# Stick-breaking decode over a paged cache: values fetched by quarter pages from GpSimd's queue, attention weights turned on TensorE

## The chip, the cores and the metric

One core of one Trainium2 chip runs the whole program. The metric is the device time of one execution in microseconds (us), median of three runs. The engines are PE (TensorE: matmuls, with PEld for its weight loads), DVE (VectorE), ACT (ScalarE), POOL (GpSimd), and SP, which here only issues DMAs. SPq, ACTq and POOLq are the queues of those engines' sequencers, from which DMAs are issued.

## The reference

One step of a hybrid decoder layer, for a prompt of 1024 tokens and for 8 samples of 8 new tokens each, whose past is 4096 tokens in a paged cache. Half of the heads do native sparse attention (NSA), the other half stick-breaking attention. The change touches the stick-breaking part of the samples alone:

```python
def stick_breaking(q, q_pos, k, v, k_pos):
    z = jnp.einsum('bqhd,bkhd->bhqk', q, k).astype(jnp.float32) * (HEAD_DIM ** -0.5)
    before = (k_pos[None, :] < q_pos[:, None])[None, None]
    log_beta = jnp.where(before, jax.nn.log_sigmoid(z), -jnp.inf)
    log_keep = jnp.where(before, jax.nn.log_sigmoid(-z), 0.0)
    log_keep_after = lax.cumsum(log_keep, axis=3, reverse=True) - log_keep
    a = jnp.exp(log_beta + log_keep_after)
    return jnp.einsum('bhqk,bkhd->bqhd', a, v.astype(jnp.float32)).astype(q.dtype)
```

`cache_sb` has 320 pages of 128 tokens; a token has 8 heads of 64 keys (2 KB) and then 8 heads of 64 values (2 KB). A sample's page table names its 32 pages, so 8 samples read 256 pages, 134 MB in all.

## The kernel before

The program goes through four stages: the projections with the prompt's stick-breaking attention (to about 590 us of the profiled span), the samples' NSA (to about 970 us), then the prompt's NSA together with the samples' stick-breaking attention (about 976 to 1520 us), and the output projections. The change lies in the third of these, in `phase_b`.

`phase_b` makes 32 steps, 4 for each sample, from the last token backwards (the cumulative sum runs in reverse, and a step hands its carry to the next). A step covers 8 pages, that is two halves `f` of four pages. Its parts are functions of the class `Step`, each with a due time in `BSTEP`, counted in steps:

- `load` (L1472): one DMA of SP for a page, keys and values together (512 KB), into a slot of the tile `bkv`. There are 8 slots for keys (`K.nkk`) and 24 for values (`K.nkv`), from the list `BC`. A load waits until both of its slots are free.
- `turn` (L1484): DVE transposes the 32x32 blocks of one page of keys (128x512) into `bkT`.
- `score` (L1491): 128 small matmul records on PE for the scores `bz` of a step, 32 columns at a time in four tile positions.
- `soft` (L1499): softplus on ACT and DVE, a scan on DVE for each half of the heads (L1507 calls L1407), the carried offsets by two matmuls into `bpt` (L1515, L1516; the PSUM pool holds one such buffer, `K.npt`), a subtraction on POOL (L1522), and the exponential on ACT (L1524).
- `out` (L1527): DVE turns the weights' 32x32 blocks (`baT`, L1531), then 16 copies of 32x128 elements, 8 on ACT and 8 on POOL, move the blocks between partition groups into `bAT` (L1539, L1541), and `av` (L1413) multiplies them with the values, page by page, into `bo`. These matmuls set the value slots free.

The prompt's NSA runs between these parts: 64 units (4 pairs of heads by 2 heads by 8 blocks of queries), each with scores on PE (L1037, L1210, L1217), a biased maximum on DVE (L1201), exponentials on ACT (L1221, L1235), three scalings by the gates (L1247), transposes on PE (L1256), copies out of PSUM on ACT (L1765) and the product with the values (L1279). `DSC` names the engine of the three scalings: "GGG" is POOL for all three, in the order selected, compressed (128x32, the tile `cz`), window. The letter list `MSB` holds no engine, so the framework orders each engine's queue in this stage by itself from the order of the program and its own estimates; on every engine the instructions then run in that order, and one that waits holds up all that is behind it. SP's queue holds the loads of all pages and a few loads and stores of the other parts.

Of the kernel before, what the change touches and what calls it, by code (L numbers as in the profile page):

```python
# [1322 lines left out]
def phase_b(K, es, psb):  # L1323

    nc, A, T = K.nc, K.A, K.T
# [57 lines left out]
    V.memset(one, 1.0)  # L1385
    vnew = cst.tile([32, 2, 512], F32, name="bvn")
# [3 lines left out]
    st = {}  # L1390
# [25 lines left out]
    carried, out, summed, count = {}, {}, [], [0]  # L1416
# [49 lines left out]
    class Step:  # L1466
# [5 lines left out]
        def load(t, i):  # L1472

            c = t.b * 32 + t.s * 8 + i
            n = count[0]
            count[0] += 1
            ks, vs = n % K.nkk, K.nkk + n % K.nkv
            t.k[i], t.v[i] = kv[:, ks], kv[:, vs]
            e = nc.sync
            with K.tc.issue_after(st[e].ins) if e in st else nullcontext():  # L1480
                r = e.value_load(pti[0:1, c:c + 1], min_val=0, max_val=319)
            st[e] = e.dma_start(kv[:, ks:vs + 1:vs - ks], cache[bass.ds(r, 1)].rearrange("o t (x c) -> (o t) x c", x=2))

        def turn(t, i):  # L1484
            f = i // 4
            if f not in t.kT:
                t.kT[f] = wT.tile([128, 16, 4, 32], F32, name="bkT", bufs=K.nkT)
            V.transpose(t.kT[f][:, :, i % 4], t.k[i].rearrange("p (j c) -> p j c", j=16))  # L1488
            t.done.append(("t", i))
# [9 lines left out]
        def soft(t):  # L1499

            assert ("s", 0) in t.done
            z, carry = t.z, carried[t.b]

            spc = wk.tile([128, 2, 257], F32, name="bs", bufs=2)
            sp = spc[:, :, 0:256]
            S_.copy(spc[:, :, 256:257], carry)
            t.a = a = wk.tile([128, 2, 256], F32, name="ba", bufs=2)  # L1507
            yield from softplus(a, sp, z)
            for g in range(2):
                scan(sp[:, g, ::-1], 256, spc[:, g, 256:257])  # L1510
            carried[t.b] = spc[:, :, 0:1]
            yield

            o = psb.tile([128, 512], F32, name="bpt", bufs=K.npt)[:, 0:16].rearrange("p (g k) -> p g k", g=2)
            nc.tensor.matmul(o, UL[0], sp[:, :, 0::32], start=True, stop=False, skip_group_check=True)  # L1515
            nc.tensor.matmul(o, UL[1], spc[:, :, 32::32], start=False, stop=True, skip_group_check=True)  # L1516
            V.tensor_tensor(a, z, sp, op=OP.subtract)
            yield
            os = wk.tile([128, 2, 8], F32, name="bos", bufs=2)
            S_.copy(os, o)  # L1520
            a4 = a.rearrange("p g (k t) -> p (g k) t", k=8)
            G.tensor_tensor(a4, a4, os.rearrange("p g k -> p (g k)").unsqueeze(2).to_broadcast([128, 16, 32]), op=OP.subtract)  # L1522
            yield
            S_.activation(a, a, AF.Exp)  # L1524
            t.done.append("w")

        def out(t):  # L1527

            assert "w" in t.done
            aT = wk.tile([128, 16, 32], F32, name="baT", bufs=1)  # L1530
            V.transpose(aT, t.a.rearrange("p g (k t) -> p (g k) t", k=8))  # L1531
            yield

            AT = wk.tile([128, 16, 4, 8], F32, name="bAT", bufs=2)
            for h in range(4):
                for x in range(4):
                    o, i = AT[x * 32:x * 32 + 32, :, h], aT[h * 32:h * 32 + 32, :, x * 8:x * 8 + 8]
                    if K.bev[(h * 4 + x) % len(K.bev)] == "A":
                        S_.copy(o, i)  # L1539
                    else:  # L1540
                        G.tensor_scalar(o, i, 1.0, 0.0, op0=OP.mult, op1=OP.add)  # L1541
            for f in (1, 0):
                yield
                for i in range(f * 4 + 3, f * 4 - 1, -1):
                    av(out[t.b // 4][:, t.b % 4], lambda g, hp: AT[:, g * 8 + i, hp * 2:hp * 2 + 2].rearrange("k h q -> k (h q)"), t.v[i],
                       False, t.s == 0 and i == 0)
                    summed.append(t.b // 4)
# [14 lines left out]
    for b in range(8):  # L1562
        g = begin(b)
        L += [(b * 4 + t, g) for t in P["b"]]
        for n in range(4):
            x = Step(b, 3 - n)
            t1 = b * 4 + n
            for m in range(8):
                L.append((t1 + P["k"][0] + m * P["k"][1], once(x.load, 7 - m)))
                L.append((t1 + P["t"][0] + m * P["t"][1], once(x.turn, 7 - m)))  # L1570
            for m in range(2):
                L.append((t1 + P["s"][m], once(x.score, 1 - m)))
            for name, g in (("w", x.soft()), ("x", x.out())):
                L += [(t1 + t, g) for t in P[name]]
# [157 lines left out]
BC = [int(x) for x in "1,1,8,24,2".split(",")]  # L1732
# [5 lines left out]
DSC = "GGG"  # L1738
# [10 lines left out]
BSTEP = {'k': [-1.2, 0.1], 't': [-0.35, 0.065], 's': [-0.08, 0.2], 'w': [0.22, 0.4, 0.56, 0.68, 0.78], 'x': [0.84, 0.9, 1.14, 1.24], 'n': [-1.6, -0.9, -0.85, -0.8, -0.78, -0.7, -0.65, -0.6], 'b': [-0.38, 1.05], 'f': [4.4]}  # L1749
# [178 lines left out]
```

## Time and profile before

| | before |
|---|---|
| median of 3 runs | 1796.08 us (1794.98 to 1798.1) |
| the profiled execution | 1797.21 us, its span 1795.4 us |
| PE busy | 1623.3 us, 90% of the span |
| DVE busy | 1233.7 us, 69% |
| ACT busy | 884.1 us, 49% |
| POOL busy | 613.5 us, 34% |

The span runs from the first to the last instruction that the profiler saw; the device time of the same execution is 1.8 us longer. Busy shares are averages over stages with different limits, so the stage of the change has to be read by itself. A group of instructions is given as line, engine, operation, output<-input, shape and count, then its busy time and the mean of one in ns, then the idle time of the engine just before and what ended it.

### The profile page before, as it was taken

Reading aid. Unit: us, or ns where it says so; the run is one execution under the profiler, and the core shown is the slowest. Engines: PE = TensorE matmul, PEld = TensorE weight load, DVE = VectorE, ACT = ScalarE, POOL = GpSimd, SP = SyncE. Lnnn points to the kernel's source line nnn. Section 1 sums busy time; section 2 is a strip of 40 time slices with the busy share of each in tenths; the row PEclk is TensorE's granted clock in tenths of the full one; section 3 lists DMA queues with packets and bytes.
Section 4 is the critical chain, followed back from the end, with each engine's and each line's share of the span. In section 5 each row is a group of like instructions: output and inputs, shape, how many; then the busy total and the mean of one; then the engine's idle time right before and its main releaser. Section 6 shows DMA issues by size and latency. Waiting matters only on the chain.

```text
span 1795.4 us, 41675 instructions
## 1 busy us (share of the span) xinstructions
PE 1623.3 (90%) x15742; PEld 1380.5 (77%) x15742; DVE 1233.7 (69%) x2892; ACT 884.1 (49%) x2220; POOL 613.5 (34%) x1057
## 2 busy tenths in 40 slices
PE   5999999999988799999998689898789898889998
PEld 5999898888876688899897466666567666677887
DVE  7336656877777578888887887877787785664322
ACT  4214645756657334444444467676567677311111
POOL 3123021121314455555553244344335444530000
PEclk9999999999987899999998699999799999799999
DMA  5235232131225455555555997876888872652210
GB/s 196 84 113 156 66 114 77 48 118 53 85 58 129 150 204 191 188 201 186 192 201 156 325 321 253 286 266 224 284 297 273 272 267 75 188 174 60 87 50 35
DMA packets 187082, 300.79 MB, mean 168 GB/s; under 512 B 30265, under 2 KB 100730, under 8 KB 178554
## 3 DMA queue, kind: packets, MB, share of 16 engines
q1 hardware_dynamic: 144930, 206.65, 35.5%
q0 software_dynamic: 9216, 67.11, 11.2%
q10 hardware_dynamic: 32736, 24.38, 4.3%
q8 instruction: 124, 2.03, 0.5%
q14 instruction: 76, 0.62, 0.1%
HBM read 271.81 MB, written 30.48 MB: 168 GB/s over the span
## 4 chain that ended last, share of the span: by engine, by line
PE 58%; DVE 14%; DMA 12%; issue 7%; ACT 5%; POOL 3%; SPq 1%; ACTq 0%; POOLq 0%; DVEq 0%
PE acc L278 12%; PE acc L1634 11%; PE H L510 6%; DMA bkv<-in_cache_sb 4%; PE bo L1413 4%; PE pt L1279 3%; DMA raw<-in_cache_nsa,cidx 3%; PE acc L276 3%; PE pt L1256 2%; PE bz L1397 2%; DVE bkT L1488 2%; PE pt L1106 2%; PE sc L682 2%; PE cav L824 1%; PE pt L1050 1%
## 5 line engine op out<-in xcount | busy, mean ns | idle before, releaser
L278 PE MATMUL acc<-whi,hh 128*128 128x256 f32 (+1 forms) x704 | 203.1, 290 | 4.1 <-DVE og L1767 2.5
L278 PE MATMUL acc<-wlo,hh 128*128 128x256 f32 (+1 forms) x704 | 200.7, 287 | 0.0
L278 PE MATMUL acc<-whi,hl 128*128 128x256 f32 (+1 forms) x704 | 199.7, 289 | 0.0
L1488 DVE STREAM_TRANSPOSE bkT<-bkv 128x512 f32<-128x512 f32 x256 | 170.4, 690 | 42.0 <-DMA bkv<-in_cache_sb 30.3
L278 PEld LDWEIGHTS acc<-whi,hh 128*128 128x128 f32 x704 | 134.5, 191 | 6.8 <-POOL whi L122 2.9
L491 ACT CAST XH<-xt 128x512 fp32r<-128x512 f32 x128 | 79.1, 618 | 121.8 <-PE H L510 111.1
L1247 POOL TENSOR_SCALAR t<-t,nst 128x640 f32<-128x640 f32 (+7 forms) x128 | 93.5, 732 | 129.5 <-DVE nst L1238 67.3
L278 PEld LDWEIGHTS acc<-wlo,hh 128*128 128x128 f32 x704 | 134.5, 191 | 0.2 <-issue 0.2
L278 PEld LDWEIGHTS acc<-whi,hl 128*128 128x128 f32 x704 | 132.3, 191 | 0.4 <-issue 0.3
L122 POOL TENSOR_SCALAR whi<-wraw 128x512 fp32r<-128x512 f32 (+1 forms) x60 | 53.8, 921 | 190.8 <-PE acc L248 154.7
L1413 PE MATMUL bo<-bkv,bAT 128*16 128x128 f32 x2048 | 93.6, 299 | 26.9 <-POOL bAT L1541 22.0
L1256 PE MATMUL pt<-idf,t 128*128 128x128 f32 x528 | 93.7, 294 | 18.0 <-ACT aT L1765 5.1
L661 POOL DMA_INDIRECT raw<-in_cache_nsa,cidx x64 | 66.9, 1045 | 102.9 <-DVE xt L486 51.1
L1541 POOL TENSOR_SCALAR bAT<-baT 32x128 f32<-32x128 f32 x256 | 75.4, 295 | 77.3 <-DVE baT L1531 54.0
L1765 ACT COPY aT<-pt 128x512 f32<-128x512 f32 (+3 forms) x167 | 77.0, 475 | 47.2 <-PE pt L1050 20.7
L1413 PEld LDWEIGHTS bo<-bkv,bAT 128*16 128x16 f32 x2048 | 62.6, 104 | 48.9 <-POOL bAT L1541 32.2
L1397 PE MATMUL bz<-bkT,bQ 128*32 128x128 f32 x2048 | 94.5, 293 | 4.0 <-DVE bkT L1488 1.3
L1256 PEld LDWEIGHTS pt<-idf,t 128*128 128x128 f32 x528 | 60.3, 146 | 44.2 <-issue 19.4
L510 PE MATMUL H<-w1hk,XH 128*128 128x256 f32 (+1 forms) x272 | 86.3, 317 | 8.6 <-ACT XH L491 7.8
L486 DVE STREAM_TRANSPOSE xt<-raw 128x512 f32<-128x512 f32 x132 | 88.1, 680 | 6.1 <-PE H L510 3.5
L1094 DVE TENSOR_TENSOR_SCAN t<-ones,t 128x1024 f32<-128x1024 f32 (+7 forms) x64 | 87.5, 1368 | 0.7
L496 POOL TENSOR_TENSOR XL<-xt,XH 128x512 fp32r<-128x512 f32 x56 | 72.1, 1287 | 37.2 <-ACT XH L491 36.6
(468 smaller groups left out, 5063.8 us busy)
## 6 DMA issues: line engine op xcount, KB each, us to landing
bkv<-in_cache_sb SPq DMA_DIRECT2D x256, 512.0 KB
wraw<-in_w_in SPq DMA_DIRECT2D x28, 512.0 KB
x<-in_x_prompt SPq DMA_DIRECT2D x8, 512.0 KB
out_sb_rows_prompt<-o ACTq DMA_DIRECT2D x32, 128.0 KB
s_gT<-og ACTq DMA_DIRECT2D x16, 256.0 KB
cwin<-in_state_win SPq DMA_DIRECT2D x8, 512.0 KB
wr<-in_w_out SPq DMA_DIRECT2D x16, 256.0 KB
u<-s_uT SPq DMA_DIRECT2D x8, 512.0 KB
```

The lines of the kernel that those rows point to most:

```text
L278: nc.tensor.matmul(acc[:, :w], a[:, k, t * 128:(t + 1) * 128], b[:, k, :w], start=i == 0, stop=i == 23)
L486: V.transpose(xt[:, :, e, :, b], raw[:, :, 0:256].rearrange("p l (k e c) -> p e l k c", e=2, c=32)[:, e])
L491: S_.copy(XH.rearrange("p a b -> p (a b)"), x.rearrange("p e k b s -> p (e k b s)"))
L510: nc.tensor.matmul(H[:m, kv * 256:kv * 256 + 256], x[:, c], y[:, l * 2 + e], start=start and l + kv + e + i == 0, stop=stop and l == 7 and ...
L1094: nc.vector.tensor_tensor_scan(a[:, ::-1], K.ones.to_broadcast([128, W]), a[:, ::-1], 0.0, op0=OP.mult, op1=OP.add)
L1247: nc.gpsimd.tensor_scalar(x, x, c, 1.0, op0=OP.mult, op1=OP.mult)
L1256: nc.tensor.transpose(pt[:, b * 128:(b + 1) * 128], x, K.id)
L1397: nc.tensor.matmul(z(h, g), q(j), kT(j), start=jj == 0, stop=jj == 1, skip_group_check=True, tile_position=(0, h * 32))
L1413: nc.tensor.matmul(oav[i * 32:i * 32 + 16], lhs(g, hp), v[:, i * 128:i * 128 + 128], start=first, stop=last, skip_group_check=True, tile_p ...
L1488: V.transpose(t.kT[f][:, :, i % 4], t.k[i].rearrange("p (j c) -> p j c", j=16))
L1634: nc.tensor.matmul(acc, a, b, start=i == 0, stop=i == len(terms) - 1)
L1765: S_.copy(o, i)
```

## The change

The page's values no longer come with its keys. SP loads only keys (256 KB a page). POOL gathers the values by indirect DMA, by quarter: one gather takes 32 tokens of each of the four pages of a half step, 128 rows of 2 KB, with row numbers computed once at the start of the stage (four small matmuls, a scaling and four DVE instructions for `vidx`). With values in that layout, the weights need a full 128x128 turn: four PE transposes a step into a `bpt` buffer and one ACT copy out of it replace the DVE turn and the 16 block copies. Keys are turned two pages at a time. One scan of 514 columns, with a mask `keep` that is zero where the second half begins, replaces two of 256. There are 12 slots for keys and 20 for values, keys are due 0.1 step earlier, values have due times of their own ("v"), and the scaling of the compressed part moves from POOL to DVE.

```diff
+    keep = cst.tile([128, 2, 257], BF, name="bkeep")
+    G.memset(keep, 1.0)
+    G.memset(keep[:, :, 256:257], 0.0)
+
+    vtab = hbm(A["cache_sb"], 0, [[512, 320 * 128 * 2], [1, 512]])
+    vidx = cst.tile([128, 4, 64], I32, name="bvi")
+    o32 = wk.tile([1, 32], F32, name="bu", bufs=2)
+    G.memset(o32, 1.0)
+    ptf = wk.tile([1, 256], F32, name="ba", bufs=2)
+    S_.copy(ptf, pti)
+    pp = psb.tile([128, 512], F32, name="bpt", bufs=K.npt)
+    for i in range(4):
+        nc.tensor.matmul(pp[i * 32:i * 32 + 32, 0:64], o32, ptf[:, i::4], start=True, stop=True, skip_group_check=True, tile_position=(0, i * 32))
+    vf = wk.tile([128, 64], F32, name="ba", bufs=2)
+    V.tensor_scalar(vf, pp[:, 0:64], 128.0, rq[:, 0:1], op0=OP.mult, op1=OP.add)
+    for x in range(4):
+        V.tensor_scalar(vidx[:, x], vf, 2.0, float(x * 64 + 1), op0=OP.mult, op1=OP.add)
...
-    carried, out, summed, count = {}, {}, [], [0]
+    carried, out, summed, count = {}, {}, [], [0, 0]
...
-            ks, vs = n % K.nkk, K.nkk + n % K.nkv
-            t.k[i], t.v[i] = kv[:, ks], kv[:, vs]
+            ks = n % K.nkk ^ 1
+            t.k[i] = ks
...
-            st[e] = e.dma_start(kv[:, ks:vs + 1:vs - ks], cache[bass.ds(r, 1)].rearrange("o t (x c) -> (o t) x c", x=2))
+            st[e] = e.dma_start(kv[:, ks], cache[bass.ds(r, 1)].rearrange("o t (x c) -> (o t) x c", x=2)[:, 0])
+
+        def values(t, m):
+
+            f, x = 1 - m // 4, m % 4
+            t.v[f, x] = v = kv[:, K.nkk + count[1] % K.nkv]
+            count[1] += 1
+            n = t.b * 8 + t.s * 2 + f
+            with K.tc.issue_after(st[G].ins) if G in st else nullcontext():
+                G.indirect_dma_start(out=v, out_offset=None, in_=vtab, in_offset=bass.IndirectOffsetOnAxis(ap=vidx[:, x, n:n + 1], axis=0))
...
-            V.transpose(t.kT[f][:, :, i % 4], t.k[i].rearrange("p (j c) -> p j c", j=16))
-            t.done.append(("t", i))
+            k = t.k[i]
+            assert i % 2 == 0 and k % 2 == 0 and t.k[i + 1] == k + 1
+            V.transpose(t.kT[f][:, :, i % 4:i % 4 + 2].rearrange("p j i t -> p i j t"), kv[:, k:k + 2].rearrange("p i (j c) -> p i j c", j=16))
+            t.done += [("t", i), ("t", i + 1)]
...
-            for g in range(2):
-                scan(sp[:, g, ::-1], 256, spc[:, g, 256:257])
+            x = spc.rearrange("p g c -> p (g c)")[:, ::-1]
+            V.tensor_tensor_scan(x, keep.rearrange("p g c -> p (g c)")[:, ::-1], x, 0.0, op0=OP.mult, op1=OP.add)
...
-            G.tensor_tensor(a4, a4, os.rearrange("p g k -> p (g k)").unsqueeze(2).to_broadcast([128, 16, 32]), op=OP.subtract)
+
+            st[G] = G.tensor_tensor(a4, a4, os.rearrange("p g k -> p (g k)").unsqueeze(2).to_broadcast([128, 16, 32]), op=OP.subtract)
...
-            aT = wk.tile([128, 16, 32], F32, name="baT", bufs=1)
-            V.transpose(aT, t.a.rearrange("p g (k t) -> p (g k) t", k=8))
-            yield
-
-            AT = wk.tile([128, 16, 4, 8], F32, name="bAT", bufs=2)
-            for h in range(4):
-                for x in range(4):
-                    o, i = AT[x * 32:x * 32 + 32, :, h], aT[h * 32:h * 32 + 32, :, x * 8:x * 8 + 8]
-                    if K.bev[(h * 4 + x) % len(K.bev)] == "A":
-                        S_.copy(o, i)
-                    else:
-                        G.tensor_scalar(o, i, 1.0, 0.0, op0=OP.mult, op1=OP.add)
+            pt = psb.tile([128, 512], F32, name="bpt", bufs=K.npt)
+            for f in (1, 0):
+                for g in range(2):
+                    c = f * 2 + g
+                    nc.tensor.transpose(pt[:, c * 128:c * 128 + 128], t.a[:, g, f * 128:f * 128 + 128], K.id)
+            yield
+
+            AT = wk.tile([128, 2, 2, 4, 4, 8], F32, name="bAT", bufs=2)
+            S_.copy(AT.rearrange("k f g x h q -> k (f g) h x q"), pt.rearrange("k (c h x q) -> k c h x q", c=4, h=4, x=4))
             for f in (1, 0):
                 yield
-                for i in range(f * 4 + 3, f * 4 - 1, -1):
-                    av(out[t.b // 4][:, t.b % 4], lambda g, hp: AT[:, g * 8 + i, hp * 2:hp * 2 + 2].rearrange("k h q -> k (h q)"), t.v[i],
-                       False, t.s == 0 and i == 0)
+                for x in range(4):
+                    av(out[t.b // 4][:, t.b % 4], lambda g, hp: AT[:, f, g, x, hp * 2:hp * 2 + 2].rearrange("k h q -> k (h q)"), t.v[f, x], False, t.s == 0 and f == 0 and x == 3)
...
-                L.append((t1 + P["t"][0] + m * P["t"][1], once(x.turn, 7 - m)))
+                L.append((t1 + P["v"][0] + m * P["v"][1], once(x.values, m)))
+                if m % 2:
+                    L.append((t1 + P["t"][0] + m * P["t"][1], once(x.turn, 7 - m)))
...
-BC = [int(x) for x in "1,1,8,24,2".split(",")]
+BC = [int(x) for x in "1,1,12,20,2".split(",")]
...
-DSC = "GGG"
+DSC = "GVG"
```

In `BSTEP`, 'k' goes from [-1.2, 0.1] to [-1.3, 0.1], and 'v': [-0.2, 0.12] is new; the other entries stay.

## Rows read from the trace of the kernel before

**Rows 1.** Busy time by stretch: whole stage, its start, two stretches with PE full:

```profile
core 0: us, PE busy (x) PEld busy (x) DVE busy (x) ACT busy (x) POOL busy (x), PEclk, DMA share, GB/s
985.00:1520.00 535.00, 454.49 (x6569) 340.60 (x6570) 416.40 (x1124) 366.36 (x1075) 221.12 (x504) 0.92 0.78 264
985.00:1060.00 75.00, 50.16 (x821) 38.07 (x824) 65.87 (x176) 39.83 (x118) 22.68 (x58) 0.75 0.99 340
1060.00:1080.00 20.00, 20.00 (x305) 14.65 (x295) 16.89 (x48) 15.86 (x44) 6.42 (x15) 1.00 0.74 252
1360.00:1400.00 40.00, 39.98 (x570) 29.59 (x569) 29.66 (x83) 29.27 (x87) 18.03 (x41) 0.99 0.89 302
```

**Rows 2.** Chain of work that ended last, 985 to 1520 us, shares by line:

```profile
by line: DMA bkv<-in_cache_sb 13.2%; PE bo L1413 11.8%; PE pt L1279 10.2%; PE pt L1256 8.2%; PE bz L1397 8.0%; DVE bkT L1488 6.8%; issue 3.9%; ACT bAT L1539 3.8%; POOL bAT L1541 3.4%; PE z L1210 3.4%; DVE t L1201 3.3%; PE z L1037 2.3%; DVE 
```

**Rows 3.** The same chain in order of time (start, us, what), 1140 to 1175 us:

```profile
1140.06 0.60 DVE baT L1531
...
1140.84 0.29 POOL bAT L1541
...
1143.34 0.31 POOL bAT L1541
1143.65 0.04 issue
1143.69 2.90 PE bo L1413 x62
...
1153.39 0.07 SPq L1482
...
1154.29 6.99 DMA bkv<-in_cache_sb
1161.28 0.02 issue
1161.31 0.71 DVE bkT L1488
```

**Rows 4.** Waits in the stage: total us, times, longest:

```profile
SPq L1482 <- PE bo L1413: 126.0, 43, 11.0
SPq L1482 <- DVE bkT L1488: 12.5, 9, 3.6
PE bo L1413 <- POOL bAT L1541: 22.0, 20, 5.5
PE bo L1413 <- ACT bAT L1539: 3.1, 5, 0.9
ACT ba L1524 <- POOL ba L1522: 8.3, 7, 3.0
```

**Rows 5.** Groups of instructions by shape, 985 to 1520 us:

```profile
L1488 DVE STREAM_TRANSPOSE bkT<-bkv 128x512 f32<-128x512 f32 x254 | 169.1, 690 | 41.9 <-DMA bkv<-in_cache_sb 30.3 <-PE bz L1397 10.7
L1256 PE MATMUL pt<-idf,t 128*128 128x128 f32 x483 | 84.4, 288 | 10.1 <-ACT aT L1765 4.6 <-ACT u L1765 1.7 <-ACT aW L1765 1.1
L1541 POOL TENSOR_SCALAR bAT<-baT 32x128 f32<-32x128 f32 x256 | 75.4, 295 | 77.3 <-DVE baT L1531 54.0 <-DVE nst L1238 6.0 <-DVE nst L1232 1.5
L1539 ACT COPY bAT<-baT 32x128 f32<-32x128 f32 x256 | 75.4, 294 | 12.4 <-DVE baT L1531 9.2
L1407 DVE TENSOR_TENSOR_SCAN bs<-bone,bs 128x256 f32<-128x256 f32 x64 | 46.1, 762 | 0.2
L1522 POOL TENSOR_TENSOR ba<-ba,bos 128x512 f32<-128x512 f32 x32 | 33.6, 1050 | 95.7 <-DVE nst L1232 31.4 <-ACT bos L1520 22.4 <-DVE ba L1517 16.6
L1765 ACT COPY aT<-pt 128x512 f32<-128x512 f32 x44 | 24.6, 578 | 13.9 <-PE pt L1256 13.7
L1531 DVE STREAM_TRANSPOSE baT<-ba 128x512 f32<-128x512 f32 x32 | 22.2, 694 | 6.9 <-ACT ba L1524 6.8
L1247 POOL TENSOR_SCALAR cz<-cz,nst 128x32 f32<-128x32 f32 x61 | 19.0, 311 | 0.0
```

**Rows 6.** DVE groups of other lines, whole span:

```profile
L715 DVE STREAM_TRANSPOSE cwT<-ckz 128x256 f32<-128x256 f32 x8 | 3.5, 437 | 0.0
L1094 DVE TENSOR_TENSOR_SCAN t<-ones,t 128x512 f32<-128x512 f32 x8 | 9.7, 1213 | 0.1
L346 DVE TENSOR_SCALAR cidf<-ptf,crv 128x32 f32<-128x32 f32 x2 | 0.8, 418 | 0.0
L347 DVE TENSOR_SCALAR cidx<-cidf 128x32 int32<-128x32 f32 x2 | 0.3, 174 | 0.0
```

**Rows 7.** Instructions of L661, the samples' NSA gather: ns min/median/max, first and last start:

```profile
L661 POOL DMA_INDIRECT raw<-in_cache_nsa,cidx x64: 937/988/2747, 568.3 to 948.4; - x64
...
DMA to landing us min/median/max: 5.6/6.0/8.2
```

More of the change, by code (lines that the diff above doesn't have):

```diff
@@ L1746 @@
 CHAIN = {'v': [-1.805], 'f': [3.581], 'q': [1.762, 2.274, 2.335, 2.335], 'k': [2.6, 2.7, 4.243, 4.243, 4.243, 4.342, 4.535, 4.559, 4.709, 4.909, 4.979, 5.109], 'w': [3.893, 4.152, 4.422], 'm': [5.22, 5.307, 5.457, 5.588, 5.688, 5.763, 5.924, 5.94, 6.122, 6.122], 's': [6.24, 6.31, 6.443, 6.443, 6.541, 6.635, 6.773, 6.935, 6.984], 'o': [6.868, 6.89, 6.977, 6.977, 7.127, 7.149, 7.151, 7.151, 7.151], 'p': [6.185, 6.243], 'z': [7.121, 7.181, 7.466, 7.643, 8.081]}
-BSTEP = {'k': [-1.2, 0.1], 't': [-0.35, 0.065], 's': [-0.08, 0.2], 'w': [0.22, 0.4, 0.56, 0.68, 0.78], 'x': [0.84, 0.9, 1.14, 1.24], 'n': [-1.6, -0.9, -0.85, -0.8, -0.78, -0.7, -0.65, -0.6], 'b': [-0.38, 1.05], 'f': [4.4]}
+BSTEP = {'k': [-1.3, 0.1], 'v': [-0.2, 0.12], 't': [-0.35, 0.065], 's': [-0.08, 0.2], 'w': [0.22, 0.4, 0.56, 0.68, 0.78], 'x': [0.84, 0.9, 1.14, 1.24], 'n': [-1.6, -0.9, -0.85, -0.8, -0.78, -0.7, -0.65, -0.6], 'b': [-0.38, 1.05], 'f': [4.4]}
 DSTEP = {'d': [0.7], 'u': [-0.021187, 0.600415, 1.110032, 1.444397], 'p0': [-2.268865, -2.1, -2.0, -1.9, -1.613669, -0.637195, -0.261999, -0.062563, -0.062463], 'p2': [-0.3, -0.25, -0.2, -0.16, -0.13, -0.1, -0.08, -0.05, -0.03], 'p': [-0.574473, -0.274473, -0.274373, -0.054473, 0.011527], 'l': [0.0, 0.104884, 0.2, 0.321272, 0.4, 0.5, 0.91108, 0.91118, 0.91128, 0.91138, 1.003464, 1.003564, 1.003664, 1.046872, 1.135437, 1.177231, 1.327231, 1.478462], 'c': [0.0, 0.0001, 0.203868, 0.283868, 0.322359, 0.372359, 0.561636, 0.561736, 0.635005, 0.801548, 0.954133, 0.954233, 0.977915, 1.009986, 1.052523, 1.052623, 1.253582, 1.311505]}
```

## The prediction

> **What bounds the kernel now.** I read the views in this order: busy time by stretch, the chain of work that ended last, the waits, the groups by shape. All that the change touches lies in one stage, from about 985 to 1520 us. There [rows 1] PE is busy 454 of 535 us, DVE 416, ACT 366, POOL 221, and the transfers take 0.78 of the DMA engines. No engine is full on average, but PE is the nearest to it, and there are stretches in which it is full: 305 records in 20 us, 570 in 40 us. Take the longer one: 14.25 records a us. The stage's 6569 records at that rate would take 461 us, so 74 of the 535 us are PE standing still or running at a lower granted clock (0.92 over the stage against 0.99 to 1.00 in the full stretches; 0.75 in the first 75 us, where PE is busy 50 us and the DMA share is 0.99).
>
> What makes PE stand still? The chain [rows 2] gives the largest single share to the transfers of `bkv`, 13.2% of 535 us, that is 71 us. In order of time [rows 3] one turn of a loop can be read: DVE turns the weights (`baT`), POOL copies blocks (from 1140.84 to 1143.65), the products `bo` run for 2.9 us, after some more work of PE the SP queue issues a load (1153.39), the transfer takes 6.99 us, and DVE turns the page the moment that it lands. The waits show why the load was late: SP stood 126 us, 43 times, for `bo` (L1413), which sets value slots free, and only 12.5 us for the turn that sets key slots free [rows 4]. So keys are late because they travel with values and wait for value slots. PE in turn waits 22.0 us for POOL's block copies and 3.1 us for ACT's [rows 4]. Both are links of the same loop.
>
> **Part by part, against the profiled execution's 1797.2 us (span 1795.4 and 1.8 around it).**
>
> *Block copies out, PE transposes in.* Removed: 32 DVE turns (22.2 us), 256 copies on ACT (75.4 us) and 256 on POOL (75.4 us) [rows 5]. Added: 128 PE transposes of 128x128 and 32 ACT copies of 128x512. The nearest row for the first is L1256, the same shape: 84.4 us for 483, 0.175 us each, so 128 x 0.175 = 22.4 us of PE [rows 5]. The nearest for the second is L1765 at 0.578 us: 32 x 0.578 = 18.5 us [rows 5], so ACT is relieved by 57 us. The path of one step shrinks from a turn and a row of eight copies (0.694 + 8 x 0.295 = 3.1 us) to four transposes and one copy (4 x 0.175 + 0.578 = 1.3 us). Of PE's 25.1 us wait for the copies I count 20 us as gone; if the new copy stood fully exposed (18.5 us) it would be 6.6, and at best 25.1. PE's 22.4 us I count in full, since PE is the fullest engine; it would be nothing if all transposes fell into gaps, and 37 us if they cost the mean of one record (0.288 us). An added wait: the transposes' `bpt` is the one buffer that the offsets also use, so the next step's two offset matmuls wait for the ACT copy, and with them what is behind on PE; by the due times in `BSTEP` the copy comes at 0.9 of a step and those matmuls at 0.56 of the next, 0.66 of a step later, so nothing is counted.
>
> *Keys without values.* SP's issue count stays 256, but a key load now waits for a turn, not for `bo`, with 12 slots instead of 8 and half the bytes before it can land. The loop above is cut. What is late next is PE's own work, since the rest of the 74 us, 74 - 25 = 49 us, is all that can be had beside the copies' wait. Nothing back, or all 49: I take half, 24 us, because the chain's 71 us of transfers speak for more, while the stage moves the same bytes at a share of 0.78 and of 0.99 at its start, where both tenants of the queue are needed early.
>
> *DVE.* Turns by pairs: widths 256 and 512 cost 0.437 and 0.690 us [rows 5, 6], so 0.184 fixed and 0.99 ns a column, and 1024 columns 1.20 us; 128 x (2 x 0.690 - 1.20) = 23 us less. One scan: 512 columns cost 1.213 against 2 x 0.762 [rows 5, 6], 32 x 0.31 = 10 us less, if the mask reads as fast as the constant. The scaling of 61 recorded `cz` (64 in all) comes from POOL, where it took 19.0 us; on DVE a 128x32 instruction took 0.174 or 0.418 us [rows 6], the latter with operands from a tile as here, so I take 0.3: 19 us more. DVE's work falls from 416 by 22 + 23 + 10 - 19 = 36 us. Only that on the chain counts: turns of keys are 6.8% of it, 36 of their 169 us [rows 2, 5], so 23 x 36/169 = 5 us. Bounds: 0 and 36, the latter if DVE were the limit.
>
> *POOL.* It loses 75.4 + 19.0 us and gets 256 gathers. The row for a gather is that of the samples' NSA: 0.988 us for 128 rows, here too 128 rows though of 2 KB in place of 8 KB [rows 7]. 256 x 0.988 = 253 us, and POOL goes from 221 to 380 of some 510 us, 74%. A gather waits until the product of 2.5 steps before has set its slot free; behind it stand the subtraction (L1522) and the gate scalings, for which ACT and PE wait. Issued from 0.2 of a step before to 0.64 after a step's start and used from 1.14 on (`BSTEP`), at some 16 us a step, it has 8 us and more to land; 1 MB took 6.0 us [rows 7]. So its landing is hidden; without that cover a step would lose up to 6 us. For the subtraction: a gather is under way about half of the time and delays it 0.5 us; today 7 of 32 are waited for by ACT [rows 4]. That gives 32 x 0.5 x 7/32 = 3.5 us, taken as 4. Below: 0. Above: the rival below.
>
> *Start.* Four small matmuls, one copy, five short DVE instructions and two memsets run while the stage before still holds PE; at some 0.3 us each they would cost 3 us if nothing covered them. Counted as 0.
>
> Sum: -20 + 22 - 24 - 5 + 4 = -23 us: 1774 for the profiled execution. The median of the runs shown lies 1.1 us under that execution, so 1773.
>
> The row of the gathers has a longest of 2.747 us beside its median of 0.988 [rows 7]: some are held up. [...]
>
> **Rivals.**
>
> 1. *The transposes eat the gain.* The loop was only one of several late things, and behind the key there is always another wait: the 24 us don't come, the rest gives -20 + 22 - 5 + 4 = +1, so about 1797, 1790 to 1803 with the terms' bounds. For it: the chain is spread over a dozen lines of PE [rows 2]. Against: SP's 126 us of waiting are concentrated on one line.
>
> 2. *POOL's queue (slower).* One mechanism: the subtraction stands behind gathers in POOL's order, and the exponential, the transposes and the products of the step wait for it. Two gathers ahead cost 1.98 us a step, 32 x 1.98 = 63 us, which turns -23 into +40: 1836. It decides from 23/32 = 0.72 us a step, one gather in three steps of four. If gathers are stretched as well, POOL itself fills: with 127 us of other work it is full in 510 us from (510 - 127)/256 = 1.5 us each, and at 2 us it needs 639 us, over 100 us more than now. For it: 74% busy in strict order. Against: POOL has half of its time free today, and at 41% only 8.3 us of ACT's waiting go to it.
>
> 3. *PE at its floor.* All 74 us come back: 461 + 22 = 483 us, 52 less, 1744. For it: full stretches exist, with all parts running. Against: in the first 75 us the DMA share is 0.99.
>
> That the change doesn't do what it says I see no way to: each removed group is named by its own line.
>
> **How the numbers follow.** The likeliest case, the loop cut and part of the slack won (1752 to 1790), gets 0.56; the floor 0.06; rival 1 0.16; rival 2 0.22. A measurement tells about 0.2%, 3.6 us, from no change, so same is 1792.5 to 1799.7. Faster: 0.56 + 0.06 + 0.04 of rival 1 = 0.66. Same: 0.09 of rival 1. Slower: 0.03 of it and 0.22 = 0.25. The range for 8 in 10 goes from 1748, which leaves out most of the floor (0.04), to 1812, which leaves out some two thirds of rival 2 (0.15).
>
> **What would show it.** Right: SP's wait for `bo` gone, DVE's wait for `bkv` (30.3 us [rows 5]) under 10; `bkv` under 6% of the chain; pairs near 1.20 us, scans near 1.22, gathers near 1 us; POOL near 75% of the stage; PE's records up by 128 while its standing still falls. Wrong: gathers over 1.5 us, ACT or PE waiting for POOL for more than 25 us, or PE's idle time as before with another releaser's name on it.

## The result, and the profile after

The changed kernel takes 1808.34 us (median of 10 runs, 1803.27 to 1816.67) against 1798.26 for the kernel before: a ratio of 1.0062, 95% interval 1.0038 to 1.0086. It is slower by 10 us where 23 us of gain were forecast; the range 1748 to 1812 holds it near its upper end. Three of the five groups of runs told below were disturbed: there, kernels that gather in their steps ran with PE standing still in a way that the other groups never show (last section), so the readings rest on the two quiet groups and on kernels without such gathers.

The profiled execution takes 1809.58 us, span 1807.8. Busy time by stretch, the stage of the change, after (columns as in [rows 1]):

```profile
985.00:1530.00 545.00, 463.59 (x6672) 350.03 (x6674) 406.63 (x994) 310.48 (x846) 385.48 (x444) 0.91 0.77 261
```

PE stands still for 545 - 464 = 81 us; before, over its 535 us, it was 81 too [rows 1]. So nothing of PE's slack was won, and PE now has the 128 transposes to do as well. POOL went from 221 to 385 us.

The waits in the stage, after (total us, times, longest):

```profile
ACT ba L1556 <- POOL ba L1554: 34.8, 15, 8.6
POOL bQ L1477 <- DMA bkv<-in_cache_sb,bvi: 30.9, 6, 6.3
PE pt L1256 <- POOL t L1247: 25.7, 10, 7.2
POOL t L1247 <- DVE nst L1238: 21.0, 8, 5.0
DVE bkT L1519 <- DMA bkv<-in_cache_sb: 7.9, 5, 2.4
PE bo L1432 <- ACT bAT L1570: 3.2, 7, 0.8
```

Set beside [rows 4, 5]: PE's 25.1 us for the block copies fell to 3.2, and DVE's 30.3 us for keys to 7.9. Both did what was forecast. In their place ACT waits 34.8 us for POOL's subtraction (8.3 before), PE 25.7 us for POOL's gate scalings, and POOL itself 30.9 us for gathers to land. This last wait was in no part of the prediction: the copies that place the next sample's queries into `bQ` (L1477, in `begin`) stand on POOL, and in the program as built they wait for the gathers in flight; why they do no run shows.

The chain of work that ended last, 985 to 1530 us, shares by line:

```profile
by line: PE bz L1416 9.8%; PE pt L1256 9.5%; PE pt L1279 9.0%; issue 7.1%; DVE bkT L1519 6.8%; DMA bkv<-in_cache_sb,bvi 6.1%; PE bo L1432 5.7%; POOL bkv L1510 4.4%; DMA bkv<-in_cache_sb 4.4%; PE z L1210 3.7%; DVE bs L1541 3.1%; DVE t L1201 
```

The loads of keys have 4.4%, from 13.2% [rows 2]. The gathers' landings have 6.1%, 33 us, and these are five pieces of 6.1 to 7.4 us, each of which ends just when the second copy into `bQ` starts. So the stops for landings lie on the chain.

The groups by shape in the stage, after (columns as in [rows 5]):

```profile
L1510 POOL DMA_INDIRECT bkv<-in_cache_sb,bvi x256 | 254.9, 996 | 74.4 <-issue 46.3 <-PE bo L1432 5.3 <-PE pt L1256 4.5
L1519 DVE STREAM_TRANSPOSE bkT<-bkv 128x1024 f32<-128x1024 f32 x126 | 150.0, 1224 | 20.5 <-PE bz L1416 12.3 <-DMA bkv<-in_cache_sb 7.9
L1541 DVE TENSOR_TENSOR_SCAN bs<-bkeep,bs 128x514 f32<-128x514 bf16 x32 | 40.4, 1262 | 0.3
L1566 PE MATMUL bpt<-idf,ba 128*128 128x128 f32 x128 | 22.7, 297 | 15.0 <-ACT ba L1556 15.0
L1245 DVE TENSOR_SCALAR cz<-cz,nst 128x32 f32<-128x32 f32 x60 | 20.9, 348 | 1.2
L1570 ACT COPY bAT<-bpt 128x512 f32<-128x512 f32 x32 | 18.7, 585 | 11.9 <-PE bpt L1566 11.7
```

Each price was met: the gather 0.996 us (0.988 forecast), the pair 1.22 (1.20), the scan 1.26 (1.22), the transposes 22.7 us (22.4), the copy 0.585 (0.578), `cz` 0.35 (0.3). What the prices don't hold is the gap from one gather to the next, 0.30 us for which the profile shows no instruction of POOL (most of them are the 46.3 us of "issue", 162 times; the rest has other names): a gather behind a gather costs 1.25 us. Before an instruction that computes there is almost no gap (1238.97 to 1239.00 below). And the gathers don't come one by one: 26 times all eight stand in a row. One step on POOL, the timeline (start, us, instruction, count, idle before):

```profile
1227.93 1.04 POOL L1554 TENSOR_TENSOR ba<-ba,bos 128x512 f32<-128x512 f32 x1
1229.13 1.04 POOL L1510 DMA_INDIRECT bkv<-in_cache_sb,bvi  x1 [0.16 <-issue]
1230.47 0.95 POOL L1510 DMA_INDIRECT bkv<-in_cache_sb,bvi  x1 [0.31 <-issue]
...
1238.02 0.95 POOL L1510 DMA_INDIRECT bkv<-in_cache_sb,bvi  x1 [0.30 <-PE bo L1432]
1239.00 0.31 POOL L1477 TENSOR_SCALAR bQ<-bQc 32x128 f32<-32x128 f32 x1
1244.27 1.00 POOL L1477 TENSOR_SCALAR bQ<-bQc 32x128 f32<-32x128 f32 x3 [4.96 <-DMA bkv<-in_cache_sb,bvi]
1245.37 2.60 POOL L1247 TENSOR_SCALAR t<-t,nst 128x256 f32<-128x256 f32 x4
1247.93 1.05 POOL L1554 TENSOR_TENSOR ba<-ba,bos 128x512 f32<-128x512 f32 x1
```

Eight gathers from 1229.13 to 1238.97, 1.25 us apart, that is 10 us in one piece; then the stop for landings; then the scalings, and only then the next step's subtraction. PE at that moment stands for a scaling that is behind the stop, from the timeline of all engines:

```profile
1245.91 0.48 PE L1256 MATMUL pt<-idf,t 128*128 128x128 f32 x1 [4.88 <-POOL t L1247]
```

### The profile page after: what moved, and what is told of

Same layout as the page of the kernel before. It is cut to its first block, busy times and chain, and to the rows that moved or that the text cites. A ratio compares the mean times of both kernels' runs of the same rounds, so it can differ in the third digit from the quotient of the medians.

```text
span 1807.8 us, 41633 instructions
## 1 busy us (share of the span) xinstructions
PE 1629.0 (90%) x15878; PEld 1388.5 (77%) x15878; DVE 1226.2 (68%) x2769; ACT 829.7 (46%) x1997; POOL 772.2 (43%) x996
## 4 chain that ended last, share of the span: by engine, by line
PE 41%; DVE 14%; DMA 9%; issue 6%; POOL 5%; ACT 2%; SPq 1%; ACTq 0%; DVEq 0%; POOLq 0%
PE acc L1664 11%; PE H L510 6%; DMA raw<-in_cache_nsa,cidx 4%; PE bz L1416 3%; PE pt L1256 3%; PE pt L1279 3%; DVE bkT L1519 2%; DMA bkv<-in_cache_sb,bvi 2%; PE bo L1432 2%; PE acc L278 1%; PE cav L824 1%; PE sc L682 1%; POOL bkv L1510 1%; DMA bkv<-in_cache_sb 1%; PE acc L276 1%
## 5 line engine op out<-in xcount | busy, mean ns | idle before, releaser
L1510 POOL DMA_INDIRECT bkv<-in_cache_sb,bvi x256 | 254.9, 996 | 74.4 <-issue 46.3
L1519 DVE STREAM_TRANSPOSE bkT<-bkv 128x1024 f32<-128x1024 f32 x128 | 152.5, 1224 | 20.5 <-PE bz L1416 12.3
L1256 PE MATMUL pt<-idf,t 128*128 128x128 f32 x528 | 99.1, 306 | 38.3 <-POOL t L1247 31.2
L1247 POOL TENSOR_SCALAR t<-t,nst 128x640 f32<-128x640 f32 (+7 forms) x128 | 98.1, 781 | 33.9 <-DVE nst L1238 21.2
L661 POOL DMA_INDIRECT raw<-in_cache_nsa,cidx x64 | 67.9, 1061 | 102.1 <-DVE xt L486 52.6
L1416 PE MATMUL bz<-bkT,bQ 128*32 128x128 f32 x2048 | 99.0, 297 | 3.9 <-DVE ba L1548 2.6
L1201 DVE CUSTOM_DVE_ANT_0 t<-z,bx 128x1024 f32<-128x1024 f32 (+7 forms) x96 | 74.2, 772 | 27.0 <-PE pt L1256 16.8
L496 POOL TENSOR_TENSOR XL<-xt,XH 128x512 fp32r<-128x512 f32 x56 | 72.2, 1289 | 38.1 <-ACT XH L491 36.5
L1432 PE MATMUL bo<-bkv,bAT 128*16 128x128 f32 x2048 | 82.0, 278 | 5.3 <-ACT bAT L1570 3.2
```

What stands on the lines that cost most here:

```text
L1247: nc.gpsimd.tensor_scalar(x, x, c, 1.0, op0=OP.mult, op1=OP.mult)
L1256: nc.tensor.transpose(pt[:, b * 128:(b + 1) * 128], x, K.id)
L1416: nc.tensor.matmul(z(h, g), q(j), kT(j), start=jj == 0, stop=jj == 1, skip_group_check=True, tile_position=(0, h * 32))
L1432: nc.tensor.matmul(oav[i * 32:i * 32 + 16], lhs(g, hp), v[:, i * 128:i * 128 + 128], start=first, stop=last, skip_group_check=True, tile_p ...
L1510: G.indirect_dma_start(out=v, out_offset=None, in_=vtab, in_offset=bass.IndirectOffsetOnAxis(ap=vidx[:, x, n:n + 1], axis=0))
L1519: V.transpose(t.kT[f][:, :, i % 4:i % 4 + 2].rearrange("p j i t -> p i j t"), kv[:, k:k + 2].rearrange("p i (j c) -> p i j c", j=16))
```

## Experiments

Times are medians beside the kernel before on the same chip (1797.4 to 1799.3).

**The DVE part alone.** The kernel before with pair turns and the single scan, nothing else:

```diff
-            V.transpose(t.kT[f][:, :, i % 4], t.k[i].rearrange("p (j c) -> p j c", j=16))
+            V.transpose(t.kT[f][:, :, i % 4:i % 4 + 2].rearrange("p j i t -> p i j t"), kv[:, k:k + 2].rearrange("p i (j c) -> p i j c", j=16))
...
-            for g in range(2):
-                scan(sp[:, g, ::-1], 256, spc[:, g, 256:257])
+            V.tensor_tensor_scan(x, keep.rearrange("p g c -> p (g c)")[:, ::-1], x, 0.0, op0=OP.mult, op1=OP.add)
```

> The kernel before with only the turns of keys by pairs and the one scan. DVE's work falls by about 33 less what the pair waits for its second page. The prediction's term: DVE hardly on the path, 5 us, 1788 to 1797 us. Rival: DVE sets the pace of the stage, 20 to 33 us come back, 1765 to 1778 us. If pairs wait for the later of two pages at a time when keys are late anyway, slower than before, 1800 us and more.

Measured 1774.2 us, ratio 0.9884 (0.9861 to 0.9908): 23.7 us faster than the 1797.9 beside it. The stage's busy times in it:

```profile
985.00:1505.00 520.00, 444.56 (x6613) 341.36 (x6613) 404.47 (x974) 366.41 (x1082) 227.79 (x509) 0.92 0.79 270
```

POOL and ACT are as busy as before; the stage is shorter by 20 us (the last weight load of `bo` starts at 1499.4 us against 1519.6). By that, DVE, at 416 of 535 us, had been nearer to the path than its share of the chain said. This is the best kernel here that computes the whole reference.

**Values by SP instead of POOL.** First in the quarter layout, one transfer a page into 32 partitions and four slots, so that the computation stays whole:

```diff
-                G.indirect_dma_start(out=v, out_offset=None, in_=vtab, in_offset=bass.IndirectOffsetOnAxis(ap=vidx[:, x, n:n + 1], axis=0))
+            st[e] = e.dma_start(kv[i * 32:i * 32 + 32, s0:s0 + 4], cache[bass.ds(r, 1)].rearrange("o (x r) (y c) -> (o r) x y c", x=4, y=2)[:, :, 1])
```

> The changed kernel with the same layout of values, but each page's values loaded by one DMA of SP (32 partitions by four quarters of 2 KB) instead of gathers on POOL; transposes on PE, pairs, scan, slots and due times stay. Theory A: all of the cost was the gathers, 1760 to 1785 us, as the prediction's terms without POOL. Theory B: transposes on PE are the cost, 1800 to 1812 us. If SP's queue takes POOL's place as the holder-up (key loads behind value loads that wait for products), SP's wait for the products is again over 60 us and the time lies near the kernel before.

Measured 1894.99, ratio 1.0536 (1.0514 to 1.0558). Then as whole pages on 128 partitions, to take the shape of the transfer out of it:

```diff
+            st[e] = e.dma_start(v, cache[bass.ds(r, 1)].rearrange("o t (x c) -> (o t) x c", x=2)[:, 1])
```

> The changed kernel with the values of all steps loaded by SP, one direct DMA of 256 KB for each of the eight slots of a step, instead of by POOL's gathers; the bytes, the slots and the due times are the same, but a slot then holds the values of one page and not a quarter of four, so the products use the wrong rows (nothing else is changed). Theory 'POOL's queue' (eight gathers of 1.25 us each, and the copies of bQ that wait for them to land, hold up the subtraction and the gate scalings behind them): POOL is relieved of some 320 us, its waits vanish, and the time falls to 1755 to 1775. Rival 'not POOL' (the PE transposes, the keys' own loads or the new order of the loads cost the time): it stays at 1800 to 1815. A loss beyond 1815 would mean that SP's queue is now the late one, with values waiting for bo ahead of keys.

Measured 1884.34, ratio 1.0478 (1.045 to 1.0507): almost as slow. And the step of the prediction that cuts keys loose from values, alone on the kernel before:

```diff
-            st[e] = e.dma_start(kv[:, ks:vs + 1:vs - ks], cache[bass.ds(r, 1)].rearrange("o t (x c) -> (o t) x c", x=2))
+            st[e] = e.dma_start(kv[:, ks], cache[bass.ds(r, 1)].rearrange("o t (x c) -> (o t) x c", x=2)[:, 0])
...
+            st[e] = e.dma_start(kv[:, vs], cache[bass.ds(r, 1)].rearrange("o t (x c) -> (o t) x c", x=2)[:, 1])
```

> The kernel before with keys and values in loads of their own, both issued by SP (512 loads of 256 KB in place of 256 of 512 KB), with the changed kernel's 12 key and 20 value slots and its due times for them; no gathers, turns and block copies as before. The prediction's step 'keys cut loose from values' alone is worth 24 us: 1774 if it holds. If the loop through the values' slots was only one of several late things: 1790 to 1800. If SP's queue in strict order makes a key wait behind a value that waits for bo: over 1800.

Measured 1898.28, ratio 1.0559 (1.053 to 1.0587). The three share one thing, 512 loads on SP, and the timeline of SP in the second shows it (start, us, instruction):

```profile
1151.56 0.34 SPq L1501 DMA_DIRECT2D bkv<-in_cache_sb  x1
1152.76 0.34 SPq L1514 DMA_DIRECT2D bkv<-in_cache_sb  x1
1153.87 0.34 SPq L1501 DMA_DIRECT2D bkv<-in_cache_sb  x1
1155.07 0.34 SPq L1514 DMA_DIRECT2D bkv<-in_cache_sb  x1
```

One load leaves every 3.51/3 = 1.17 us, with no wait in between: before each the page's number is read into a register and turned into an address (a register load of 0.27 us, its arithmetic, the DMA's own 0.34 us, and short gaps between them). 512 x 1.17 = 599 us, more than the stage of 535. That values hold up keys by waiting for `bo`, the other cause that was expected, is not it: SP's waits for `bo` in the second run are 5.8 us in all. The two theories about values and keys can't be told apart by these runs; what they show is that SP's queue can't issue both, so that gathers on POOL, or one load for both, are what there is to choose from.

**Half of the gathers** (`half_sp`). Every second value slot by SP (as whole pages, so half of the products use the wrong rows), 384 loads on SP and four gathers a step on POOL; the edit is that of the second of the runs above, under `if m % 2:`.

> As the run before, but only every second value slot is loaded by SP: four gathers a step stay on POOL, which alternate with four direct loads (these hold whole pages, so half of the products use the wrong rows). Theory 'POOL's queue': a dose between, 1775 to 1795. Rival 'not POOL': 1800 to 1815, as with all gathers.

> Four gathers and four direct value loads a step (whole pages in the direct slots, so that half of the products use the wrong rows), loaded once more. Theory 'it belongs to the program': 1764 to 1774 again. Rival 'it belongs to the load': it may come at 1815 to 1840 like half_unpair and half_true.

Measured 1765.81, ratio 0.9837 (0.9804 to 0.9871), and 1763.98 on another chip. The changed kernel itself beside the second of these:

> The changed kernel itself, loaded once more. In some runs with gathers (the copies of bQ moved to ACT or DVE, half_unpair, half_true) PE puts out one record every 0.7 to 1.4 us during gather bursts though nothing that the profile shows holds it, and the chain names an unknown releaser; in others (the changed kernel, half_sp) it never does. Theory 'it belongs to the program': 1803 to 1817 as before, with no such stretch. Rival 'it belongs to the load of a program on a chip, not to the program': this kernel can show it now, and be 1830 or more.

Measured 1806.67, ratio 1.0055 (1.0027 to 1.0083). So halving the gathers is worth 1806.67 - 1763.98 = 42.7 us, more than the dose that was expected. Busy times and waits with half of them (second run):

```profile
985.00:1490.00 505.00, 448.73 (x6558) 343.64 (x6552) 398.08 (x983) 306.92 (x840) 253.67 (x312) 0.93 0.84 278
```

```profile
ACT ba L1563 <- POOL ba L1561: 16.3, 13, 2.6
PE pt L1256 <- POOL t L1247: 6.4, 6, 2.3
POOL bQ L1477 <- DMA bkv<-in_cache_sb,bvi: 21.9, 7, 4.9
```

ACT's wait for the subtraction halves, PE's for the scalings falls from 25.7 to 6.4 us, and PE's standing still from 81 to 56 us. The transposes, the ACT copy and the keys' own loads are all still there, so none of them accounts for the 42.7 us. The gathers' share and that of the stops for landings can't be parted here: the stops fell too, from 30.9 to 21.9 us.

**The copies of `bQ` off POOL.** The changed kernel, all eight gathers:

```diff
-            G.tensor_scalar(Qb[b % 2][x * 32:x * 32 + 32, :, x * 8:x * 8 + 8], Qc[x * 32:x * 32 + 32, :, b * 8:b * 8 + 8], 1.0, 0.0, op0=OP.mult, op1=OP.add)
+            S_.copy(Qb[b % 2][x * 32:x * 32 + 32, :, x * 8:x * 8 + 8], Qc[x * 32:x * 32 + 32, :, b * 8:b * 8 + 8])
```

> The changed kernel with the four copies of each sample's queries (L1477) on ACT in place of POOL. In the changed kernel POOL stands 30.9 us there until gathers issued just before have landed. Theory A, POOL's queue is what makes the change slow: those stops lie on the path, 15 to 30 us come back, 1778 to 1793 us, ratio to the kernel before 0.989 to 0.997. Theory B, the added work and waits of PE (four transposes a step behind the exponential) are what costs: POOL's stops are hidden, within 4 us of the changed kernel, about 1808 us, ratio 1.004 to 1.008.

> The changed kernel with the copies of bQ on ACT, loaded once more. Theory 'it belongs to the program': 1996 to 2013 again, with PE's slow records. Rival 'it belongs to the load': it may come without them, and then shows what removing the 30.9 us stop of POOL is worth: 1775 to 1800.

The first time 2001.37, ratio 1.1127 (1.1104 to 1.115), in a disturbed group; the second time, undisturbed, 1782.98, ratio 0.994 (0.9919 to 0.996). Beside the changed kernel of the same group that is 1806.67 - 1782.98 = 23.7 us, for copies that took 7.2 us themselves in the stage. Waits in the second:

```profile
ACT ba L1556 <- POOL ba L1554: 20.7, 13, 3.3
PE pt L1256 <- POOL t L1247: 15.2, 12, 3.2
```

The stop for landings is gone and with it the long waits: the longest that ACT stands for POOL is 3.3 us, from 8.6. The landings have left the chain (985 to 1510 us):

```profile
by line: PE bz L1416 13.2%; PE pt L1256 10.3%; PE pt L1279 10.2%; PE bo L1432 7.3%; issue 6.2%; DVE bkT L1519 4.6%; PE z L1210 4.2%; DVE bs L1541 3.1%; POOL t L1247 2.8%; DVE t L1201 2.5%; POOL bkv L1510 2.1%; PE bpt L1566 2.0%; PE z L1037 
```

They had 33 us of it before, and 23.7 came back.

**Half of the gathers, whole computation** (`half_true`). The first half of a step's pages by SP in the quarter layout, the other by four gathers; the transfer is that of the first SP run:

> The changed kernel with the values of a step's first half of pages loaded by SP, page by page, into 32 partitions and four slots (the quarter layout that the products need), and the four gathers of the other half on POOL; the computation is whole. Theory 'POOL's queue': 1760 to 1780, as half_sp, if a transfer into 32 partitions isn't much slower than one into 128; SP then issues 384 loads, at 1.16 us each 445 us, which fits into the stage. If such transfers are slow: 1790 or more, with the products waiting for bkv.

> The same with the direct loads in the quarter layout (the computation is whole), loaded once more. Theory 'it belongs to the program': 1830 to 1842 again, with PE's slow records. Rival 'it belongs to the load': it may come without them at 1765 to 1785, as half_sp did.

1833.29 (disturbed), then 1802.96, ratio 1.0035 (1.0013 to 1.0057). SP issues as many loads as in the run with whole pages, and yet it is 39 us slower. The stage:

```profile
985.00:1520.00 535.00, 454.92 (x6514) 349.87 (x6505) 394.49 (x977) 306.77 (x837) 252.88 (x309) 0.91 1.00 261
```

The DMA engines are busy all the time and move 261 GB/s, where with whole pages a share of 0.84 moved 278: by bytes per share, the transfers into 32 partitions were the dearer ones in these two runs. DVE waits 49.4 us for keys, 28 times.

**How much the order of the queues does by itself: not measured.** The rate by which the prompt NSA's due times are scaled, moved by 0.2%:

```diff
-BRATE = float("0.9441283460447858")
+BRATE = float("0.946")
```

> The changed kernel with the rate by which the due times of the prompt's NSA are scaled moved by 0.2% (BRATE 0.9441 to 0.946): the same instructions, but the framework puts each engine's queue in a slightly different order. It measures how much of a difference the order alone can make. Both theories: within 8 us of the changed kernel (1800 to 1816). If it is off by 20 us or more, the order of the queues is a cause of the same size as the change itself.

Measured 1808.86, ratio 1.0061 (1.0036 to 1.0086): the same as the changed kernel. But the traces show that the edit did not do what was expected of it: from 976 us on, POOL's, ACT's and DVE's instructions stand, by line and tile, in exactly the order that they have in the changed kernel. The run is the changed kernel once more, and says nothing of the order. The experiments above do change it, because the framework orders the queues anew for every program: with the copies of `bQ` on ACT, about a quarter of DVE's instructions stand elsewhere in their queue. So part of the 24, the 43 and the 23.7 us can be the order that came with the edit. Against it speak the sizes, of which two lie where they were expected (15 to 30 us for the stops, 20 to 33 by the rival for DVE), and the chain, which names the landings in the one kernel and not in the other.

**Runs that were disturbed, and tell nothing of the change.** The edits: the copies of `bQ` and the two large gate scalings on ACT (`DSC = "AVA"`); those copies on DVE (`V.tensor_scalar` in place of `G.tensor_scalar`); half of the gathers (as whole pages) with those copies on ACT; half of the gathers, likewise, with page turns and two scans (`half_unpair`); the changed kernel with page turns and two scans; the copies on ACT with the subtraction on DVE.

> The changed kernel with the query copies and the two large gate scalings on ACT (the compressed one stays on DVE), so that POOL does only gathers and the subtraction of the offsets. POOL is relieved of 31 us of stops and 86 us of scalings in a stage of 545 us. Theory A: POOL's queue no longer sets the pace, PE's and ACT's waits for POOL (90 us together in the changed kernel) fall under 30, 1765 to 1785 us. Theory B: no better than the first experiment by more than 4 us, or 1800 us and above, since ACT gets 86 us more and PE keeps its transposes.

> The changed kernel, all eight gathers on POOL, with the copies of bQ on DVE instead of POOL (DVE has 407 of 545 us busy, 32 copies of some 0.3 us are 10 us). Theory 'ACT is the burden' for the slowness of the run with the copies on ACT: on DVE it is gone, and the time falls to 1775 to 1800, because POOL no longer stands for the landing (30.9 us). Theory 'eight gathers a step without a stop': as slow as with the copies on ACT, 1950 or more.

> Four gathers and four direct value loads a step (as in the run half_sp, with whole pages in the direct slots, so that half of the products use the wrong rows), and the copies of bQ on ACT instead of POOL. Theory 'the copies of bQ on ACT are the burden' (ACT's order or its longer queue): it is again far slower, 1950 or more. Theory 'eight gathers a step without a stop for their landing': with four gathers the slowness doesn't come, and the time stays within 10 us of half_sp (1756 to 1776).

> half_sp (four gathers and four direct value loads a step, half of the products with the wrong rows) with the part of the change that lies on DVE undone: keys turned page by page, one scan for each half of the heads. Theory 'the parts add up': the pairs and the single scan were worth 24 us on the kernel before, so it goes to 1785 to 1795. Rival 'DVE no longer matters once values and block copies are off the path': 1766 to 1775.

> The changed kernel with its DVE part undone: keys turned page by page, one scan for each half of the heads; all else as changed. Theory 'POOL's queue paces the stage, and DVE's work beside it is hidden': DVE's 33 us more (pairs 1.22 against 2 x 0.69 us, scan 1.26 against 2 x 0.76 us) cost little: 1805 to 1818. Rival 'the parts add up': the pairs and the single scan brought 24 us on the kernel before, so it goes to 1825 to 1835, and gathers with PE transposes alone are 30 us slower than before. If PE shows its slow single records, 1850 or more, and the run says nothing.

> The changed kernel with the copies of bQ on ACT and the subtraction of the carried offsets on DVE instead of POOL (32 x 1.05 us less on POOL, some 32 x 0.69 us more on DVE; nothing of the softmax waits behind gathers any longer, only the gate scalings do). Theory 'POOL's queue': ACT's 20.7 us wait for the subtraction goes, against the run with the copies of bQ on ACT alone (1783): 1765 to 1778. Rival 'DVE is as near to its limit': no better than 1783, or worse. If PE shows its slow single records, 1900 or more, and the run says nothing.

Measured in this order: 2033.19, 2019.54, 1825.73, 1833.13, 2024.21 and 1958.43 us. That the copies on DVE are as slow as on ACT was first read as the harm of POOL running without a stop; the later run took that reading away, since the same kernel with the copies on ACT then came at 1783.

## Why the prediction was wrong

*Block copies out:* right. PE's wait went from 25.1 to 3.2 us; 20 were counted.

*Transposes in:* right in price, 22.7 us. They wait 15.0 us for the exponential, five times up to 8.1 us, which in turn waits for POOL.

*Keys without values:* the mechanism was right (SP no longer waits for `bo`, the loads fell from 13.2% [rows 2] to 4.4% of the chain, with 6.1% for the gathers, DVE's wait to 7.9 us), but the 24 us of PE's slack that should have followed did not come: PE stands still as long as before, now 25.7 us for POOL directly and 15.0 us for the exponential behind POOL's subtraction. What the step is worth by itself no run shows, because it takes 512 loads, and at 1.17 us each these fill SP's queue for 599 us, longer than the stage.

*DVE:* the term was mis-sized. Counted at 5 us, measured at 23.7 alone on the kernel before. The step that failed is the weighing by the turns' share of the chain, "23 x 36/169": it took DVE's saving to count only where a turn stood on the chain. The prediction's own savings of these two edits, 23 + 10 = 33 us in full, lay nearer. This error goes the other way than the result: by itself it would have made the change better than forecast.

*POOL:* this is the step that failed, and with it the sign. "A gather is under way about half of the time and delays it 0.5 us" took the gathers as spread evenly, and counted 4 us. The runs showed in its place: gathers eight in a row, 1.25 us each with the gap behind them, so that what comes next waits up to 10 us and not half a gather; gate scalings that PE waits for, which were named as queued behind the gathers and priced at nothing; and the copies of `bQ`, which were not looked at, holding POOL until the gathers have landed. The last is 24 us by itself (1806.7 against 1783.0), and half of the gathers with part of that stop 43 us (1806.7 against 1764.0). "So its landing is hidden" was right for the products, for which no wait on a gather is recorded, and wrong for these copies. What the waits for the subtraction and the scalings are worth by themselves no run shows, because the runs that took them off POOL were disturbed.

Two of the prediction's own signs of being wrong came: ACT and PE wait for POOL for more than 25 us, and PE's idle time is as before under other names.

Rival 2 was the right mechanism: it named the subtraction behind gathers, and a point of decision at 0.72 us a step. ACT's wait grew by 34.8 - 8.3 = 26.5 us, 0.83 us a step. Its 1836 was too high: only 15 of 32 subtractions are waited for, and DVE gave more than was counted. POOL itself never filled, and the gathers were hardly stretched: median 0.947 us, mean 0.996, longest 1.921.

The prediction saw that some gathers are held up. The traces show what ran beside them. Of the 256 gathers 16 took over 1.1 us, and all 16 started while DVE's scan was running, which reads two tiles, its mask and its data; they ended 0.75 to 0.83 us after it. Gathers that had started before a scan did took no longer than the rest (17 of them, 0.942 to 1.023 us; 0.942 to 1.058 for the 219 that met no scan). One of the 16, from the timeline of all engines:

```profile
1256.67 1.23 DVE L1541 TENSOR_TENSOR_SCAN bs<-bkeep,bs 128x514 f32<-128x514 bf16 x1
1256.74 1.92 POOL L1510 DMA_INDIRECT bkv<-in_cache_sb,bvi  x1 [0.30 <-PE bo L1432]
```

In the kernel before, all five of the 64 gathers over 1.1 us, the longest of 2.747 among them, ran beside a `TENSOR_TENSOR` of DVE on two tiles (L446, L496). So gathers do get held up, but the 16 are 9.5 us above the median in all, in a stage of 545: that is not what cost the time. The `cz` scaling, a tensor_scalar on DVE since the change, shows no sign of holding them up in this trace: 32 gathers ran beside one, the three of them that took over 1.1 us (1.32, 1.79 and 1.84) ran beside a scan too, and the 27 that met no scan took 0.942 to 1.058 us. Why a scan of two tiles goes with long gathers no run shows.

The sum with the sizes that were measured: the whole change is +9 to +10 us, the DVE part -24, so gathers, transposes and the keys' own loads together are some 33 us worse than what they replace, if the parts add. That they add is not shown: the runs meant for it were disturbed.

## What to carry to other kernels

Before moving DMAs onto an engine that also computes, write down its queue for one step in order, and price the longest run of DMAs and not the mean: here what is behind a run of eight waits for all eight, 10 us. Look for every instruction on that engine that must wait for landings, also those that come once in four steps. And where one change bundles a gain with a loss, run the parts: two edits on DVE alone beat the bundle by some 33 us (1774.2 against 1806.7 and 1808.3). And before a run is used to show that something does not matter, see in its trace that the edit changed it.

## What the runs showed of the hardware

- In the changed kernel a gather of 128 rows of 2 KB occupied POOL for 0.947 us in the median and was followed by 0.30 us before the next. One of 128 rows of 8 KB took 0.988 [rows 7], so between these two POOL's time hardly went by bytes. Of the 20 gathers that started while DVE ran a scan of two tiles, 16 took over 1.1 us, up to 1.92, and these ended 0.75 to 0.83 us after the scan. The changed kernel's gathers landed 6.5 us after their issue in the median.
- In the run with whole pages by SP, one load whose address is read from a table was issued every 1.17 us. The register load among its steps took 0.268 us in the median, 0.262 at the least, and the DMA's own instruction 0.338 in the median.
- The disturbance. In three groups of runs, on three chips, all eight kernels that gather in their steps showed PE putting out single records 0.7 to 1.4 us apart in the later part of a run of gathers, with nothing that the profile shows to hold them: between 985 and 1700 us such idle time of PE is 24 to 125 us in these eight, and at most 4.4 us in every other trace. From the timeline of the changed kernel with the copies on ACT (first time):

```profile
1213.58 0.31 PE L1279 MATMUL pt<-aW,vw 128*64 128x128 f32 x1 [0.45 <-issue]
1214.99 0.27 PE L1279 MATMUL pt<-aW,vw 128*64 128x128 f32 x1 [1.10 <-issue]
1216.42 0.27 PE L1279 MATMUL pt<-aW,vw 128*64 128x128 f32 x1 [1.17 <-issue]
```

  In two other groups no kernel showed it, on one of the same chips and on another; the kernel before and those without gathers in their steps never did. It goes with the number of gathers: the same kernel took 2001 and then 1783 us with eight a step, 1833 and then 1803 with four. For these two kernels it is a property of the occasion and not of the program; the changed kernel itself was never run in such a group. The cause stays open. In several of these runs the chain names an unknown releaser (13% of it from 1060 to 1700 us in the first); what that releaser is no run shows.
